# Bank evictions issued inside the projection, PSUM tiles of their own for the routing tables, and a branch hint

## The chip, the cores and the metric

One Trainium2 chip, of which the kernel uses one core. The metric is the device time of one execution in microseconds. The core's engines run side by side, each with its own instruction stream in program order: TensorE (PE, matmul; PEld is its weight load), VectorE (DVE), ScalarE (ACT), GpSimd (POOL) and SyncE (SP, which here issues most DMA transfers). An engine waits for another one on semaphores.

## The reference

One layer on 512 tokens of width 1024: a mixer (gated linear recurrence in four heads beside a convolution of 31 taps), then a mixture of 16 experts of which two are chosen for each token.

```python
u = _modulate(x, sh1, sc1)
# mixer: one input projection into q, f, i, og, ca, cgt (512 columns each)
q, f, i, og, ca, cgt = jnp.split(u @ w_in + b_in, [H, 2 * H, 3 * H, 4 * H, 4 * H + C], axis=-1)
o = _hgrn2(q, f, i, lb)                      # silu(q); chunks of 64, decays exp(cumsum log f)
h_a = rmsnorm(o) * norm_w * silu(og)
a = conv31(ca * sigmoid(cgt)) + conv_b       # causal, channel by channel
h_b = silu(_layernorm(a) * conv_g + conv_bb)
x = _post_ln(ALPHA * x + g1 * (concat(h_a, h_b) @ w_out + b_out), ln1_g[l], ln1_b[l])
# experts: router, one group of four per token, top-2 inside it, SwiGLU
x = _post_ln(ALPHA * x + g2 * _moe(_modulate(x, sh2, sc2), ...), ln2_g[l], ln2_b[l])
```

## The kernel before

**The mixer** (`mixer`, L993) is written by hand in program order for every engine. Six projections `project(gi)` (L1194) of 512 columns each run one behind the other, in the order ca, cgt, f, q (gi = 3), the values i (gi = 4) and the gate og (gi = 5). A projection is four steps of 24 matmuls (128x128 by 512 columns) into four accumulators `pj`, and there are four `pj` banks in all. So the first matmul of a projection's accumulator m waits until the result of the projection before has left bank m. For gi = 3 that is the SiLU on ACT (L1341), for gi = 4 the addition of a bias on VectorE (L1429): four instructions each, both issued when `project` has returned.

Between the steps other work is issued: `between(st)` behind each step (for gi = 4 `values`, which calls `decays(st)`, L1347, the exponentials of head st and the scaled q and k of head st - 1, and two products of the conditioning matrix, `more_ada`; for gi = 5 `heads(st)`, L1494: scores with predicated copies on VectorE, states, three `more_ada`). After it `fill` (L1183) issues convolution taps. VectorE has 23 taps for each of four channel groups and one sum behind each group, ACT and POOL share 8 more. `fill` decides by counters: `Load` (L976) adds an assumed cost to each engine's counter at each instruction, and taps are issued while VectorE's counter is a given distance behind TensorE's:

```python
        v.at = max(v.at, pe.at - 8.0)
        while dve and (n > 0 or v.at < pe.at - ahead):
            dve.pop(0)()
            n -= 1
```

`ahead` is 1.5, or 5 for steps 2 and 3 of gi = 4 (`AHEAD`, L910). At the end of `project` VectorE's and ACT's counters are set to at least TensorE's (L1201). What is left of the taps is issued by `fill(200)` (L1560).

**The branch.** Behind the second head, `check` computes a flag, and `heads(2)` calls `general` (L1862), which reads the flag into a register on four engines and jumps over a slow exact computation of the scores if the flag is 0. With these inputs it is 0.

**The tables.** Behind the mixer, `moe` (L462) computes on TensorE and VectorE the tables that say which token goes to which slot (`router.tables`, L280, `weight_tables`, L315, `small`, L219), and beside them expert 0's first product (`between`, L508, into `pg`). All this uses four PSUM tiles `pz` of two banks each: the tables take turns in the four banks of `pz0` and `pz1`, `pg` and `pt` are the two halves of `pz2`, `ph` and `po` those of `pz3`. The framework keeps order between instructions by tile. `turned_rows` (L481) transposes the next rows into `pt`, and `modulate` (L336) reads them. Then one block with code of its own for each engine and hand-written semaphores runs the experts (from L572), on the same tiles. TensorE's part begins with two semaphore increments (L576), register loads (`load`, L582) and a mark (`mark`, L606) for which SP's weight loads wait.

Of the kernel before, what the change touches and what calls it, by code (L numbers as in the profile page):

```python
# [458 lines left out]
        return (w[bass.ds(at, 1), :, :].rearrange("o r n -> (o r) n") for w in self.w)  # L459


def moe(nc, tc, K, work, psum, W, n2d, zd, out):  # L462


    v, g, s, pe = nc.vector, nc.gpsimd, nc.scalar, nc.tensor
    st = K.st
    z, y, skip = ([W.gu(x, t) for t in range(4)] for x in (16, 17, 15))
    whole, lower, upper = slice(0, D), slice(0, 512), slice(512, D)

    pz = [psum.tile([128, 2, 512], F32, name=f"pz{t}", bufs=1) for t in range(4)]  # L470
    pg = pz[2][:, 0, :].rearrange("p (u n) -> p u n", u=2)
    pt = pz[2][:, 1, :].rearrange("p (c h r) -> p c h r", c=4, h=2)
    ph, po = pz[3][:, 0, :], pz[3][:, 1, :]
    n2h = n2d.rearrange("t (h c) -> (t h) c", h=2)

    def gather(i, to):
# [32 lines left out]
        for k in todo.get(i, ()):  # L509
            up(pe, W.gu(0, k), st.XT0, 2, k)  # L510

    banks = [pz[t][:, i, :] for t in range(2) for i in range(2)]

    def bank():
        banks.append(banks.pop(0))
        return banks[-1]

    with tc.manual_schedule():

        v.memset(ph, 0.0)  # L520
        K.router.tables(bank, between)
        gather(1, st.XS)
        K.router.weight_tables(bank)
        s.activation(st.SL, pg[:, 0, :], AF.Silu)
        v.tensor_tensor(st.HB, pg[:, 1, :], st.SL, op=OP.mult)
        turned_rows()
        modulate(v, K, st.XT, pt)
        K.router.small(bank)

    names = ["u", "s", "e", "v", "t", "h", "pv", "pg", "x", "g", "xf", "d", "o", "z", "fg", "fd", "zl", "ln", "v2"]  # L530
    names += [f"ga{i}" for i in range(2)] + [f"sc{i}" for i in range(3)]

    names += ["ob", "fp", "fa", "fm", "fq", "fw", "fr", "fc", "fk", "fo", "fb", "st"] + [f"z{t}" for t in range(4)]
    sem = {n: tc.alloc_semaphore("moe_" + n) for n in names}

    full_g = [[tc.alloc_semaphore(f"moe_g{i}{k}") for k in range(4)] for i in range(3)]
# [35 lines left out]
    with tc.tile_critical():  # L572
        with nc.Block() as block:  # L573
            @block.tensor
            def _(pe):
                pe.sem_inc(sem["e"], 1)  # L576
                pe.sem_inc(sem["x"], 1)

                rows = [pe.alloc_register(f"moe_rows{i}") for i in range(3)]

                def load(x, at):
                    pe.reg_load(rows[x % 3], K.cnt[0:1, at:at + 1] if isinstance(at, int) else K.cnt[0:1, bass.ds(at, 1)])  # L582
# [118 lines left out]

            @block.vector
            def _(v):
                def turned():
                    take(v, "t")
                    v.tensor_copy(st.hT, ph[:, 0:256]).then_inc(sem["h"], 1)  # L706
# [200 lines left out]
SH = (0, -1, -1)  # L907
PR = 2
WARM = 12
AHEAD = {(4, 3): 5, (4, 2): 5}  # L910
W4 = 3
WB = 3
NACT = 8
# [57 lines left out]
def col(K, nm, i):  # L971
    c = K.c0[nm] + i
    return K.cols[:, c:c + 1]
# [19 lines left out]
def mixer(nc, tc, K, I, psum, P, modd, spill, n2d, zd):  # L993
# [197 lines left out]
        while act and act[0].m <= summed[0] + 1 and s.at < pe.at and g.at < pe.at:  # L1191
            act.pop(0)()

    def project(gi, channel_major, between=None, within=None):  # L1194
        out = [pj() for _ in range(4)]
        for st in range(4):
            step(gi * 4 + st, out, channel_major, within)
            if between:
                between(st)
            fill(0, AHEAD.get((gi, st), 1.5))  # L1200
        v.at = max(v.at, pe.at)  # L1201
        s.at = max(s.at, pe.at)
        return out
# [132 lines left out]
            v.tensor_tensor_scan(f_, K.smask, a_, 0.0, op0=OP.mult, op1=OP.add)  # L1336
            bs.append(f_.rearrange("p (c i) -> p c i", c=NCH))

    pq = project(3, True, between=logs)
    for h in range(4):  # L1340
        s.activation(q_[h], pq[h], AF.Silu, bias=col(K, "b_in", h))  # L1341
    dec = P[0].tile([128, 4, NCH], F32, name="dec")
    ext = P[0].tile([128, 4, 2, NCH], F32, name="ext")

# [79 lines left out]
    SC = q4pair(2, 3)  # L1424
    for h in range(4):
        g.memset(SC[h], 0.0)
    pv = project(4, False, between=values)
    for t, p in enumerate(pv):
        v.tensor_tensor(vt[t], p, vbias[0], op=OP.add)  # L1429
    decays(4)  # L1430

    exm = P[0].tile([128, 1], F32, name="exm")
# [33 lines left out]
    def turned(h):  # L1466
        pk = ms()
        for t in range(4):
            sl = slice(t * 128, (t + 1) * 128)
            pe.transpose(pk[:, sl], X[:, 4 + h, sl], K.ident)  # L1470
        kTs[h] = t2()
        s.activation(kTs[h], pk, AF.Copy)
# [21 lines left out]
    def heads(st):  # L1494
        if st == 2:
            general(nc, tc, K, ms, bad, spill, SC, t2)
        turned(st)
        if st < 2:
            scores(2 * st)
            scores(2 * st + 1)  # L1500
        if st == 1:
            check()
        fill(4)
        states(st)
        more_ada((3, 3, 3, 2)[st])
# [356 lines left out]
def general(nc, tc, K, ms, bad, spill, SC, t2):  # L1862
# [2 lines left out]

    v, g, s, pe = nc.vector, nc.gpsimd, nc.scalar, nc.tensor
    flag = nc.values_load(bad[0:1, 0:1], engines=(ET.PE, ET.Activation, ET.DVE, ET.Pool), min_val=0, max_val=1)
    with tc.If(flag > 0):  # L1868
        for h in range(4):
            v.memset(SC[h], 0.0)  # L1870
        for h in range(4):
# [53 lines left out]
def hybrid(tc, ctx, I, out):  # L1925
# [29 lines left out]
    with tc.tile_pool(name="tb", bufs=1, reuse_waits="tile") as tb, tc.tile_pool(name="wp", bufs=1, side="right", reuse_waits="tile") as wp:  # L1955
        moe_tables(K, tb)
        nc.gpsimd.dma_start(K.g2q, bass.AP(tensor=modd.tensor, offset=modd.offset + 2 * 512, ap=[[256, 4], [0, 32], [1, 256]]))
        nc.gpsimd.dma_start(K.g2h, bass.AP(tensor=modd.tensor, offset=modd.offset + 2 * 512, ap=[[512, 2], [0, 64], [1, 512]]))
        W = Weights(nc, K, wp, X4, I["w_gate"][0], I["w_up"][0], I["w_down"][0])
        with tc.manual_schedule():  # L1960
            for x in range(3):
                W.static(x)
            nc.sync.dma_start(K.st.ln2g, bcast_rows(I["ln2_g"], D))
            nc.sync.dma_start(K.st.ln2b, bcast_rows(I["ln2_b"], D))
        with tc.tile_pool(name="mp", bufs=1, space=PSUM, reuse_waits="tile") as mp, tc.tile_pool(name="mw", bufs=1, reuse_waits="tile") as mw:
            moe(nc, tc, K, mw, mp, W, n2d, zd, out)

# [1 line left out]
_INS = ["x", "c", "ada_w", "ada_b", "w_in", "b_in", "hgrn_norm_w", "conv_w", "conv_b", "conv_ln_g", "conv_ln_b",  # L1969
# [22 lines left out]
```

## Time and profile before

| | us |
|---|---|
| median of 3 runs | 696.8 (695.91 to 701.67) |
| the profiled execution | 703.01 |
| its span, first to last instruction | 701.2 |
| TensorE busy in the span | 588.2 (84%) |
| VectorE busy | 349.2 (50%) |
| GpSimd busy | 254.5 (36%) |
| ScalarE busy | 167.0 (24%) |

All times in the rows are those of the one profiled execution, from its first instruction on. A busy share over the whole span says little here, since the stages have different limits: the mixer's projections run from 21 to about 228 us, the output projection until 330, router and tables until 388, the experts until 692. What is read is which engine waits in a stage, and what ended the wait.

### The profile page before, as it was taken

Reading aid. Unit: us, or ns where it says so; the run is one execution under the profiler, and the core shown is the slowest. Engines: PE = TensorE matmul, PEld = TensorE weight load, DVE = VectorE, ACT = ScalarE, POOL = GpSimd, SP = SyncE. Lnnn points to the kernel's source line nnn. Section 1 sums busy time; section 2 is a strip of 40 time slices with the busy share of each in tenths; the row PEclk is TensorE's granted clock in tenths of the full one; section 3 lists DMA queues with packets and bytes.
Section 4 is the critical chain, followed back from the end, with each engine's and each line's share of the span. In section 5 each row is a group of like instructions: output and inputs, shape, how many; then the busy total and the mean of one; then the engine's idle time right before and its main releaser. Section 6 shows DMA issues by size and latency. Waiting matters only on the chain. (4 is left out here: it accounts for less than half of the span.)

```text
span 701.2 us, 10474 instructions
## 1 busy us (share of the span) xinstructions
PE 588.2 (84%) x3499; PEld 319.1 (46%) x3500; DVE 349.2 (50%) x694; ACT 167.0 (24%) x253; POOL 254.5 (36%) x209
## 2 busy tenths in 40 slices
PE   4899999793996787998765888999997799999970
PEld 2578878562664344676522243333332233343430
DVE  6447587999467665577764131222221122321356
ACT  1433567542310214224501010101010010110112
POOL 2245695977620222365600232222222112132215
PEclk9999999897988678899886799999998999999985
DMA  8953223595234567769990799973799997699953
GB/s 279 356 180 121 91 91 98 164 340 179 76 119 156 178 212 275 252 226 302 395 330 28 275 341 381 378 279 60 239 371 390 382 376 265 166 379 384 344 157 120
DMA packets 78784, 170.68 MB, mean 243 GB/s; under 512 B 8866, under 2 KB 18031, under 8 KB 78718
## 3 DMA queue, kind: packets, MB, share of 16 engines
q1 hardware_dynamic: 69456, 149.19, 59.8%
q0 software_dynamic: 9136, 20.80, 10.9%
q8 instruction: 22, 0.36, 0.2%
q14 instruction: 28, 0.23, 0.1%
q10 hardware_dynamic: 142, 0.09, 0.0%
HBM read 154.96 MB, written 15.34 MB: 243 GB/s over the span
## 5 line engine op out<-in xcount | busy, mean ns | idle before, releaser
L819 POOL DMA_INDIRECT zd<-flat,dst x25 | 39.9, 1597 | 204.2 <-POOLq L541 195.8
L492 PE MATMUL pz<-wt,flat 128*32 128x256 f32 (+1 forms) x672 | 93.9, 493 | 6.1 <-PEq L541 5.9
L989 POOL TENSOR_TENSOR wL<-w,wH 128x1024 fp32r<-128x1024 f32 x30 | 74.4, 2483 | 58.1 <-ACT wH L989 58.1
L989 PE MATMUL pj<-wH,U 128*128 128x512 f32 x224 | 76.7, 414 | 16.2 <-DVE q L989 10.9
L501 PE MATMUL pz<-wt,flat 128*64 128x512 f32 (+1 forms) x544 | 84.0, 515 | 2.6 <-PEq L541 1.7
L989 PE MATMUL pj<-U,wH 128*128 128x512 f32 x256 | 81.0, 395 | 4.5 <-DVE U L989 3.0
L492 PE MATMUL pz<-R,flat 128*64 128x512 f32 (+1 forms) x416 | 77.3, 547 | 7.8 <-PEq L541 6.3
L989 DVE SCALAR_TENSOR_TENSOR mx<-R,convw,mx 128x512 f32<-128x512 f32 x88 | 66.4, 754 | 6.2 <-DVEq L1868 3.5
L679 ACT ACTIVATE flat<-pz 128x256 f32<-128x256 f32 x25 | 9.6, 384 | 239.8 <-ACTq L541 239.8
L989 PEld LDWEIGHTS pj<-wH,U 128*128 128x128 f32 x224 | 44.4, 198 | 36.0 <-issue 21.3
L492 PEld LDWEIGHTS pz<-wt,flat 128*32 128x32 f32 (+1 forms) x672 | 32.7, 125 | 51.3 <-issue 45.8
L989 PEld LDWEIGHTS pj<-U,wH 128*128 128x128 f32 x256 | 47.6, 188 | 17.0 <-DVE U L989 4.4
L711 DVE TENSOR_TENSOR flat<-pz,flat 128x256 f32<-128x256 f32 x25 | 10.6, 425 | 88.6 <-DVEq L541 82.6
L706 DVE COPY flat<-pz 128x256 f32<-128x256 f32 x26 | 11.1, 425 | 81.0 <-DVEq L541 61.1
L989 PE MATMUL pj<-U,wL 128*128 128x512 f32 x128 | 50.1, 392 | 0.0
L501 PEld LDWEIGHTS pz<-wt,flat 128*64 128x64 f32 (+1 forms) x544 | 27.4, 128 | 44.1 <-issue 40.4
L478 POOL DMA_INDIRECT flat<-n2d,idx_i x28 | 27.8, 994 | 48.7 <-DVE flat L264 23.1
L989 PE MATMUL pj<-wL,U 128*128 128x512 f32 x112 | 45.4, 405 | 0.0
L492 PEld LDWEIGHTS pz<-R,flat 128*64 128x64 f32 (+1 forms) x416 | 24.8, 131 | 44.1 <-issue 42.2
L989 POOL TENSOR_TENSOR R<-R 128x512 f32<-128x512 f32 x28 | 39.0, 1396 | 14.3 <-ACT R L989 12.9
L989 ACT ACTIVATE wH<-w 128x1024 fp32r<-128x1024 f32 x30 | 31.5, 1055 | 24.7 <-PE pj L989 11.4
L726 DVE SCALAR_TENSOR_TENSOR flat<-pz,X,g2h 128x512 f32<-128x512 f32 x18 | 13.5, 751 | 38.5 <-DVEq L541 38.5
(389 smaller groups left out, 816.2 us busy)
## 6 DMA issues: line engine op xcount, KB each, us to landing
wt<-in_w_down_dram SPq DMA_DIRECT2D x60, 512.0 KB, 7.2
wt<-in_w_gate_dram SPq DMA_DIRECT2D x80, 256.0 KB, 6.7
wt<-in_w_up_dram SPq DMA_DIRECT2D x80, 256.0 KB, 7.0
q<-in_ada_w_dram SPq DMA_DIRECT2D x28, 512.0 KB, 7.7
w<-in_w_in_dram SPq DMA_DIRECT2D x24, 512.0 KB, 3.8
aw<-in_ada_w_dram SPq DMA_DIRECT2D x20, 512.0 KB, 5.6
R<-in_w_gate_dram SPq DMA_DIRECT2D x40, 256.0 KB, 6.3
R<-in_w_up_dram SPq DMA_DIRECT2D x40, 256.0 KB, 6.0
```

Source lines behind the costliest of these rows:

```text
L478: return g.indirect_dma_start(out=to, out_offset=None, in_=n2h, in_offset=bass.IndirectOffsetOnAxis(ap=K.idx[:, i:i + 1], axis=0))
L492: i = eng.matmul(pg[m * j:m * j + m, :, 0:cw], xT[:, c, h, 0:m], w[:, :, cw * j:cw * j + cw], start=k == 0, stop=k == 7)
L501: i = eng.matmul(po[m * q:m * q + m, 0:dw], st.hT[:, c * 128 + j * m:c * 128 + j * m + m], W.dn(x, f)[:, dw * q:dw * q + dw], start=f == 0 ...
L679: s.activation(st.SL, pg[:, 0, :], AF.Silu).then_inc(sem["s"], 1)
L706: v.tensor_copy(st.hT, ph[:, 0:256]).then_inc(sem["h"], 1)
L711: v.tensor_tensor(st.HB, pg[:, 1, :], st.SL, op=OP.mult).then_inc(sem["e"], 1)
L726: v.scalar_tensor_tensor(st.o[j % 3][:, :256 * n], po[:, :256 * n], w[:, j:j + 1], g2, op0=OP.mult, op1=OP.mult).then_inc(sem["o"], 1)
L819: g.indirect_dma_start(out=zd.rearrange("r (q c) -> (r q) c", c=dw), out_offset=bass.IndirectOffsetOnAxis(ap=dst[:, j:j + 1], axis=0), in_ ...
L989: return f(out, *a, **k)
```

## The change

It has five parts. `project` takes a function `last`, called behind the matmuls of step 3 and ahead of `between` and `fill`; the four SiLUs of gi = 3 (`take_q`) and the four additions of gi = 4 (`take_v`) are passed in so. The distance 5 for step 2 of gi = 4 goes, so that step has 1.5. The branch of `general` gets a label, and on TensorE and VectorE a hint is written behind `turned(1)` that its jump is likely taken. The tables get a PSUM pool of their own that is closed behind them, with a one-bank tile each for `pg`, `pt` and two for the tables in turn; the eight banks `pz` for the experts come from a new pool behind it. The memset of `ph` moves from the head of the tables into VectorE's part of the block, with one more for the bank of `pg`, and TensorE waits for both (`pw`) ahead of its register loads.

```diff
--- before.py
+++ after.py
@@ -459,18 +459,17 @@
         return (w[bass.ds(at, 1), :, :].rearrange("o r n -> (o r) n") for w in self.w)
 
 
-def moe(nc, tc, K, work, psum, W, n2d, zd, out):
+def moe(nc, tc, K, ctx, work, W, n2d, zd, out):
 
 
     v, g, s, pe = nc.vector, nc.gpsimd, nc.scalar, nc.tensor
     st = K.st
     z, y, skip = ([W.gu(x, t) for t in range(4)] for x in (16, 17, 15))
     whole, lower, upper = slice(0, D), slice(0, 512), slice(512, D)
-
-    pz = [psum.tile([128, 2, 512], F32, name=f"pz{t}", bufs=1) for t in range(4)]
-    pg = pz[2][:, 0, :].rearrange("p (u n) -> p u n", u=2)
-    pt = pz[2][:, 1, :].rearrange("p (c h r) -> p c h r", c=4, h=2)
-    ph, po = pz[3][:, 0, :], pz[3][:, 1, :]
+    first = ExitStack()
+    psum = first.enter_context(tc.tile_pool(name="mp", bufs=1, space=PSUM, reuse_waits="tile"))
+    pg = psum.tile([128, 2, 256], F32, name="pg", bufs=1)
+    pt = psum.tile([128, 4, 2, 64], F32, name="pt", bufs=1)
     n2h = n2d.rearrange("t (h c) -> (t h) c", h=2)
 
     def gather(i, to):
@@ -509,15 +508,8 @@
         for k in todo.get(i, ()):
             up(pe, W.gu(0, k), st.XT0, 2, k)
 
-    banks = [pz[t][:, i, :] for t in range(2) for i in range(2)]
-
-    def bank():
-        banks.append(banks.pop(0))
-        return banks[-1]
-
+    bank = lambda: psum.tile([128, 512], F32, name="tbl", bufs=2)
     with tc.manual_schedule():
-
-        v.memset(ph, 0.0)
         K.router.tables(bank, between)
         gather(1, st.XS)
         K.router.weight_tables(bank)
@@ -526,11 +518,18 @@
         turned_rows()
         modulate(v, K, st.XT, pt)
         K.router.small(bank)
+    first.close()
+
+    psum = ctx.enter_context(tc.tile_pool(name="mq", bufs=1, space=PSUM))
+    pz = [psum.tile([128, 2, 512], F32, name=f"pz{t}", bufs=1) for t in range(4)]
+    pg = pz[2][:, 0, :].rearrange("p (u n) -> p u n", u=2)
+    pt = pz[2][:, 1, :].rearrange("p (c h r) -> p c h r", c=4, h=2)
+    ph, po = pz[3][:, 0, :], pz[3][:, 1, :]
 
     names = ["u", "s", "e", "v", "t", "h", "pv", "pg", "x", "g", "xf", "d", "o", "z", "fg", "fd", "zl", "ln", "v2"]
     names += [f"ga{i}" for i in range(2)] + [f"sc{i}" for i in range(3)]
 
-    names += ["ob", "fp", "fa", "fm", "fq", "fw", "fr", "fc", "fk", "fo", "fb", "st"] + [f"z{t}" for t in range(4)]
+    names += ["ob", "fp", "fa", "fm", "fq", "fw", "fr", "fc", "fk", "fo", "fb", "st", "pw"] + [f"z{t}" for t in range(4)]
     sem = {n: tc.alloc_semaphore("moe_" + n) for n in names}
 
     full_g = [[tc.alloc_semaphore(f"moe_g{i}{k}") for k in range(4)] for i in range(3)]
@@ -577,6 +576,8 @@
                 pe.sem_inc(sem["x"], 1)
 
                 rows = [pe.alloc_register(f"moe_rows{i}") for i in range(3)]
+
+                take(pe, "pw")
 
                 def load(x, at):
                     pe.reg_load(rows[x % 3], K.cnt[0:1, at:at + 1] if isinstance(at, int) else K.cnt[0:1, bass.ds(at, 1)])
@@ -701,6 +702,10 @@
 
             @block.vector
             def _(v):
+
+                v.memset(ph, 0.0)
+                v.memset(pz[2][:, 0, :], 0.0).then_inc(sem["pw"], 1)
+
                 def turned():
                     take(v, "t")
                     v.tensor_copy(st.hT, ph[:, 0:256]).then_inc(sem["h"], 1)
@@ -907,7 +912,7 @@
 SH = (0, -1, -1)
 PR = 2
 WARM = 12
-AHEAD = {(4, 3): 5, (4, 2): 5}
+AHEAD = {(4, 3): 5}
 W4 = 3
 WB = 3
 NACT = 8
@@ -1191,10 +1196,13 @@
         while act and act[0].m <= summed[0] + 1 and s.at < pe.at and g.at < pe.at:
             act.pop(0)()
 
-    def project(gi, channel_major, between=None, within=None):
+    def project(gi, channel_major, between=None, within=None, last=None):
+
         out = [pj() for _ in range(4)]
         for st in range(4):
             step(gi * 4 + st, out, channel_major, within)
+            if st == 3 and last:
+                last(out)
             if between:
                 between(st)
             fill(0, AHEAD.get((gi, st), 1.5))
@@ -1336,9 +1344,11 @@
             v.tensor_tensor_scan(f_, K.smask, a_, 0.0, op0=OP.mult, op1=OP.add)
             bs.append(f_.rearrange("p (c i) -> p c i", c=NCH))
 
-    pq = project(3, True, between=logs)
-    for h in range(4):
-        s.activation(q_[h], pq[h], AF.Silu, bias=col(K, "b_in", h))
+    def take_q(pq):
+        for h in range(4):
+            s.activation(q_[h], pq[h], AF.Silu, bias=col(K, "b_in", h))
+
+    project(3, True, between=logs, last=take_q)
     dec = P[0].tile([128, 4, NCH], F32, name="dec")
     ext = P[0].tile([128, 4, 2, NCH], F32, name="ext")
 
@@ -1424,9 +1434,12 @@
     SC = q4pair(2, 3)
     for h in range(4):
         g.memset(SC[h], 0.0)
-    pv = project(4, False, between=values)
-    for t, p in enumerate(pv):
-        v.tensor_tensor(vt[t], p, vbias[0], op=OP.add)
+
+    def take_v(pv):
+        for t, p in enumerate(pv):
+            v.tensor_tensor(vt[t], p, vbias[0], op=OP.add)
+
+    project(4, False, between=values, last=take_v)
     decays(4)
 
     exm = P[0].tile([128, 1], F32, name="exm")
@@ -1495,6 +1508,8 @@
         if st == 2:
             general(nc, tc, K, ms, bad, spill, SC, t2)
         turned(st)
+        if st == 1:
+            tc.mark_branch_hint_location("general", "LikelyTaken", engines=[ET.PE, ET.DVE])
         if st < 2:
             scores(2 * st)
             scores(2 * st + 1)
@@ -1865,7 +1880,7 @@
 
     v, g, s, pe = nc.vector, nc.gpsimd, nc.scalar, nc.tensor
     flag = nc.values_load(bad[0:1, 0:1], engines=(ET.PE, ET.Activation, ET.DVE, ET.Pool), min_val=0, max_val=1)
-    with tc.If(flag > 0):
+    with tc.If(flag > 0, label="general"):
         for h in range(4):
             v.memset(SC[h], 0.0)
         for h in range(4):
@@ -1962,8 +1977,8 @@
                 W.static(x)
             nc.sync.dma_start(K.st.ln2g, bcast_rows(I["ln2_g"], D))
             nc.sync.dma_start(K.st.ln2b, bcast_rows(I["ln2_b"], D))
-        with tc.tile_pool(name="mp", bufs=1, space=PSUM, reuse_waits="tile") as mp, tc.tile_pool(name="mw", bufs=1, reuse_waits="tile") as mw:
-            moe(nc, tc, K, mw, mp, W, n2d, zd, out)
+        with ExitStack() as st, tc.tile_pool(name="mw", bufs=1, reuse_waits="tile") as mw:
+            moe(nc, tc, K, st, mw, W, n2d, zd, out)
 
 # ---- launch: one core; inputs and outputs as the reference has them ----
 _INS = ["x", "c", "ada_w", "ada_b", "w_in", "b_in", "hgrn_norm_w", "conv_w", "conv_b", "conv_ln_g", "conv_ln_b",
```

## Rows read from the trace of the kernel before

**Rows 1.** Stretch: us; busy of PE, PEld, DVE, ACT, POOL; clock; DMA.

```profile
160.00:170.90 10.90, 0.02 (x1) 0.05 (x1) 10.76 (x13) 3.95 (x6) 10.80 (x8) 0.71 0.58 198
```

**Rows 2.** TensorE's timeline: start, us, instruction, [idle before, what ended it].

```profile
170.88 0.76 PE L989 MATMUL pj<-wH,U 128*128 128x512 f32 x1 [10.91 <-DVE q L989]
216.77 1.09 PE L989 MATMUL ms<-ident,X 128*128 128x128 f32 x4 [4.97 <-DVEq L1868]
233.25 0.55 PE L989 MATMUL mx<-q,t 64*128 64x128 f32 x1 [4.54 <-DVE cv L989]
235.23 1.93 PE L989 MATMUL pa<-aw,cc 128*32 128x512 f32 x8
```

**Rows 3.** VectorE's timeline, 155 to 182 us.

```profile
155.72 1.54 DVE L989 SCALAR_TENSOR_TENSOR mx<-R,convw,mx 128x512 f32<-128x512 f32 x2
166.24 3.91 DVE L989 SCALAR_TENSOR_TENSOR mx<-R,convw,mx 128x512 f32<-128x512 f32 x5
170.05 2.48 DVE L989 TENSOR_TENSOR q<-pj,bb 128x512 f32<-128x512 f32 x4
172.52 1.29 DVE L989 TENSOR_TENSOR q<-q,t 128x512 f32<-128x512 f32 x2
181.00 1.00 DVE L989 COPY_PREDICATED q<-R,ms 128x128 f32<-128x128 uint8 x4 [7.19 <-PE ms L989]
```

**Rows 4.** ACT's timeline around the SiLUs of q.

```profile
125.05 1.32 ACT L989 ACTIVATE R<-R,convw 128x512 f32<-128x512 f32 x2
127.92 2.41 ACT L989 ACTIVATE q<-pj,cols 128x512 f32<-128x512 f32 x4
```

**Rows 5.** VectorE's timeline, 196 to 233 us.

```profile
196.93 1.00 DVE L989 COPY_PREDICATED q<-R,ms 128x128 f32<-128x128 uint8 x4 [6.95 <-PE ms L989]
216.72 6.30 DVE L989 SCALAR_TENSOR_TENSOR mx<-R,convw,mx 128x512 f32<-128x512 f32 x8 [3.50 <-DVEq L1868]
226.02 6.29 DVE L989 SCALAR_TENSOR_TENSOR mx<-R,convw,mx 128x512 f32<-128x512 f32 x8
```

**Rows 6.** The branch's line, sequencers (q): count, ns, first and last start.

```profile
L1868 ACTq COMPARE_BRANCH  x1: 45/45/45, 202.0 to 202.0; - x1
L1868 ACTq EVENT_SEMAPHORE  x1: 17/17/17, 202.5 to 202.5; - x1
L1868 PEldq COMPARE_BRANCH  x1: 6685/6685/6685, 208.5 to 208.5; - x1
L1868 DVEq COMPARE_BRANCH  x1: 72/72/72, 213.1 to 213.1; - x1
L1868 DVEq EVENT_SEMAPHORE  x1: 21/21/21, 216.6 to 216.6; - x1
```

**Rows 7.** Short stretches: columns as in rows 1, the clock third from the end.

```profile
170.00:172.00 2.00, 1.12 (x3) 0.95 (x4) 2.00 (x5) 0.00 (x0) 1.69 (x1) 0.50 0.55 131
230.00:232.00 2.00, 0.00 (x0) 0.00 (x0) 1.93 (x3) 0.70 (x1) 1.56 (x3) 1.00 0.17 34
234.00:236.00 2.00, 2.00 (x16) 1.20 (x16) 0.63 (x2) 0.00 (x0) 0.00 (x0) 0.50 0.96 264
```

**Rows 8.** Timelines of VectorE and TensorE in the tables.

```profile
361.51 0.48 DVE L520 MEMSET pz<- 128x512 f32 x1
374.81 0.69 DVE L276 TENSOR_TENSOR flat<-flat 128x512 bf16<-128x512 f16 x1
376.45 1.41 PE L322 MATMUL pz<-flat 128*64 128x32 f16 x24 [2.65 <-DVE flat L312]
381.38 1.12 PE L483 MATMUL pz<-ident,flat 128*128 128x128 f32 x4 [2.55 <-DVE flat L525]
382.53 0.69 DVE L339 TENSOR_TENSOR flat<-pz,scT 128x512 f32<-128x512 f32 x1 [1.21 <-PE pz L483]
```

**Rows 9.** Register loads at the block's entry, columns as in rows 6.

```profile
L548 DVEq TENSOR_LOAD <-cnt_i x1: 325/325/325, 386.2 to 386.2; - x1
L582 PEldq TENSOR_LOAD <-cnt_i x16: 298/306/320, 386.5 to 663.0; - x16
```

## The prediction

> **What bounds the kernel now.** I read the table of stretches first. In the stretch behind the mixer's fifth projection TensorE is busy 0.02 of 10.90 us while VectorE is busy 10.76 [rows 1]. So there the kernel waits for VectorE, not for arithmetic on TensorE. TensorE's own timeline then names what ends its long pauses: 10.91 us by a VectorE write of `q`, 4.97 us by VectorE's queue at the branch, 4.54 us by the last convolution sum `cv` [rows 2]. All three are VectorE, so I read VectorE's timeline last. In [rows 3] the reader sees the order that causes the first pause: two convolution taps (155.72), then `decays(3)` until 166.24, five more taps, and only at 170.05 the four additions `q<-pj,bb` that empty the four `pj` banks. TensorE starts 0.83 us behind the first of them. Behind them VectorE runs out of work until 181.00.
>
> **The plan of the taps.** `fill` decides by counters how many taps are issued behind each step, so the change moves taps too. I replayed the counters by hand with their costs from the code: a tap 0.662, a step 24 x 0.215 = 5.16, an `ada_mul` 1.29, `decays` 1.64 for h = 0 and 3.12 after, all counters 0 at the start of project(4). Behind steps 0 to 3 the matmul counter stands at 7.74, 15.48, 23.22, 30.96, and the rule (stop 1.5 short, 5 short for the last two) gives 7, 7, 2, 5 items; for the last, VectorE's counter is lifted to 30.96 - 8 = 22.96 first. The trace has the 2 [rows 3], and the tap that ends before 170.05 is the fifth. With the change step 2 stops 1.5 short: 17.15 to 21.72, 7 items. At step 3 the four additions (2.65) and `decays(3)` are counted before `fill`: 21.78 + 2.65 + 3.12 = 27.55, over 25.96: 0 items. So the sum stays 7, but all stand ahead of the additions and `decays(3)` stands behind them.
>
> **Part 1, `take_v`: 8.9 us.** The additions now stand behind 7 taps that start at 155.72. A tap takes 6.29 / 8 = 0.786 us [rows 5], so 155.72 + 5.50 = 161.2 instead of 170.05 [rows 3]. TensorE starts at 162.0 instead of 170.88 [rows 2]: 8.9 us. What is late next: the same work, `decays(3)` and `decays(4)`, is now behind the additions, and queued behind it are the predicated copies of `scores(0)`, for which TensorE waits in `states(0)`. Before, all of it was over at 172.52 + 1.29 = 173.8; the amount of work is the same, so 173.8 is the late bound. The copies, at 181.00 before, would be wanted at 172.1. At the late bound that costs 1.7 us for the first, so 7.2 is the lower end. The upper end is about 11: TensorE's clock stands at 0.50 in 170 to 172, behind the long pause [rows 7], and a shorter pause may spare up to 2 us of that first step. I take 8.9, because `decays(3)` now has idle time in front of its late users.
>
> **Part 2, four taps into idle time: 3.1 us.** At the end of a group VectorE's counter is set level with TensorE's. Before, the additions were counted after that; now they are not, so in project(5) the counter is 2.65 lower. In `heads(0)` it reads 39.26 where `fill` runs up to 41.56: 4 taps, where before it read 41.91 and issued none. They land where VectorE waited 6.95 us for TensorE (the pause before 196.93, [rows 5]): cost nothing while that pause lasts, 3.1 us if it were gone. Later counters are level again, so the 4 taps are missing at the end of the list, among the eight at 226.02 [rows 5]. TensorE waited 4.54 us for the sum behind those eight [rows 2], so 4 x 0.786 = 3.1 us are gained, bounds 0 and 4.5.
>
> **Part 3, the hint: 3.0 us.** The flag is 0, so every engine jumps over the body of `general`. ACT's branch stands at 202.0 and its next event at 202.5; VectorE's branch takes 72 ns at 213.1 and its next event stands at 216.6; TensorE's branch takes 6.7 us [rows 6]. I read the two long ones as waits for the code behind the jump. They end within the pause of 3.50 us on VectorE [rows 5], and TensorE, held until 216.77 [rows 2], is released by VectorE. If the code is there in time, VectorE's pause becomes ACT's 0.5 us: 3.0 us. VectorE works from there to the sum of the last tap, so this passes on whole, and TensorE's 6.7 us started at 208.5 and must be cut as well, or it holds `turned(2)` until 215.2, which TensorE's later slack covers in part. Bounds: 0 and 3.5. The instruction that writes the hint is not in this trace; an event instruction of 17 or 21 ns is the nearest row [rows 6], so it is nothing. [...]
>
> **Part 4, the clock: 1.9 us.** [...] So `states(3)` and two ada products, 233.25 to 237.16 [rows 2], run at half speed after a pause of 4.54 us. With parts 2 and 3 that pause is about 1 us, and this work falls where the clock was still up: half of 3.9 us. Bounds 0 and 7 (the slow stretch goes on behind these rows). I take 1.9, the row that the pause is nearest to.
>
> **Part 5, the tables: 1.7 us.** The memset of `ph` leaves VectorE's chain (0.48 us long, the next starts 0.4 later): 0.4 [rows 8]. The weight tables' matmul waited 2.65 us, to the end of L312, which reads the other bank of the same tile; its own input is ready when L276 ends, 374.81 + 0.69 = 375.5, so it starts 0.9 earlier. `turned_rows` (L483) waited 2.55 us for L525, which reads the other half of `pz2`; with `pg` and `pt` apart it is done early, and VectorE's 1.21 us of waiting for it at L339 goes [rows 8]. Together 2.5. Against it stands the new wait `pw`: VectorE enters the block at 386.2 and needs 0.4 + 0.48 us for the two memsets, so TensorE may go on at about 387.1; its first register load stood at 386.5 [rows 9]. Queued behind that wait are all of TensorE's loads and the first mark, for which SP's expert loads wait. Later by 0.6, with the semaphore 0.8. Net 1.7, bounds 0 and 2.5.
>
> **Part 6, `take_q`: 0.** The four SiLUs go ahead of the convolution copies on ACT: 125.05 instead of 127.92 [rows 4], so project(4) starts 2.9 us earlier, and SP's spill of `q` and the ada loads behind it too. It hides behind VectorE: the additions at 161.2 depend on VectorE's list alone, and TensorE had finished before that. If that cover were gone it would be worth 2.9.
>
> **The sum.** 8.9 + 3.1 + 3.0 + 1.9 + 1.7 = 18.6 us. Behind 260 us I see nothing with a time of its own: the experts' loads from the fourth on start on TensorE's mark in the block, so they move along with it. Span 701.2 - 18.6 = 682.6; the profiled execution 703.0 becomes 684.4. That execution was 6.2 us above the median of 696.8, so the median becomes 678.2.
>
> **The rivals.**
> [...]
> *The gain of part 1 is taken back*: VectorE becomes the bound of project(5), because `decays(3)` under load runs on past 173.8 (it took 9 us before, from the end of two taps near 157.2 to 166.24 [rows 3]) and the four taps of part 2 then stand in TensorE's way. Parts 1 and 2 shrink from 12.0 to some 3: about 687. The pause up to 181.00 speaks against it.
> *The clock gives more*: the slow stretch behind 233 comes out half fast and the step at 162 as well, 7 us more: 671.
> [...]
>
> **Chances.** All terms as told 0.50 (own range 674 to 683); hint without effect 0.20; more from the clock 0.10; gain taken back 0.15; slower 0.05. The likeliest gives 678.2. The range runs from 670 to 688, leaving out the slower case, part of the taken-back one and the tail of the clock. One per cent, about what a measurement here can tell from no change, is 7 us: below 689.8 is faster. The first three cases and two thirds of the fourth lie there: 0.85; within one per cent 0.10; slower 0.05.
>
> **What the changed kernel's profile would show.** Part 1: TensorE's pause before project(5) ends at about 162 with the additions directly behind seven taps. Part 2: four taps behind the first `states`, and four taps instead of eight ahead of the last sum. Part 3: VectorE's pause at the branch of 0.5 us, and TensorE's branch far below 6.7. Part 4: clock 1.00 at `states(3)`. Part 5: no wait for L312 and L525, and a wait of TensorE at the new `take` of about 0.8. The prediction is wrong if the copies of `scores(0)` wait for VectorE by more than 2 us, or if the span between the last sum and the first expert grows.

## The result and the profile after

| kernel | median us | lowest to highest | runs |
|---|---|---|---|
| before, beside the changed kernel | 696.36 | 694.16 to 701.67 | 4 |
| changed | 675.28 | 674.49 to 675.74 | 4 |
| changed, second time on another occasion | 674.32 | 673.77 to 675.86 | 6 |

The ratio to the kernel before is 0.9685 (0.963 to 0.9741), the second time 0.9704 (0.9667 to 0.9741): about 21 us faster. The profiled execution took 675.64 us, its span 673.9. Against the 703.01 us of the profiled execution before that is 27.4 us, 6 more than the medians give. So the kernel before was profiled a second time, unchanged (`e0_before`): 693.67 us, span 691.9. What differs between those two profiles of one kernel is no effect of the change, and the stretches below are taken from the second one.

TensorE's timeline of the changed kernel (start, us, instruction, [idle before, what ended it]), beside [rows 2]:

```profile
126.24 0.50 PE L994 MATMUL pj<-wH,U 128*128 128x512 f32 x1 [2.04 <-ACT q L994]
162.47 0.76 PE L994 MATMUL pj<-wH,U 128*128 128x512 f32 x1 [3.54 <-DVE q L994]
207.09 0.63 PE L994 MATMUL ms<-ident,X 128*128 128x128 f32 x4 [2.12 <-DVEq L1883]
220.41 0.34 PE L994 MATMUL mx<-q,t 64*128 64x128 f32 x1 [2.15 <-DVE cv L994]
```

The first row is the start of project(4); the other three are the pauses of [rows 2]. They are there again, ended by the same three writers, and each is shorter: 3.54 us instead of 10.91 ahead of project(5), 2.12 instead of 4.97 at the branch, 2.15 instead of 4.54 ahead of `states(3)`. VectorE's timeline shows why, beside [rows 3, 5]:

```profile
156.24 5.50 DVE L994 SCALAR_TENSOR_TENSOR mx<-R,convw,mx 128x512 f32<-128x512 f32 x7
161.64 2.48 DVE L994 TENSOR_TENSOR q<-pj,bb 128x512 f32<-128x512 f32 x4
173.28 1.00 DVE L994 COPY_PREDICATED q<-R,ms 128x128 f32<-128x128 uint8 x4 [4.14 <-PE ms L994]
182.48 3.12 DVE L994 SCALAR_TENSOR_TENSOR mx<-R,convw,mx 128x512 f32<-128x512 f32 x4
190.13 1.00 DVE L994 COPY_PREDICATED q<-R,ms 128x128 f32<-128x128 uint8 x4 [4.53 <-PE ms L994]
207.04 6.30 DVE L994 SCALAR_TENSOR_TENSOR mx<-R,convw,mx 128x512 f32<-128x512 f32 x8 [0.59 <-DVEq L1883]
216.34 3.12 DVE L994 SCALAR_TENSOR_TENSOR mx<-R,convw,mx 128x512 f32<-128x512 f32 x4
```

The additions stand directly behind seven taps. Four taps have moved to 182.48, ahead of a wait for TensorE, and four instead of eight are left at 216.34. The pause at the branch is 0.59 us instead of 3.50.

Where the time went, stretch by stretch, from the second profile of each kernel. Each stretch runs from one marked instruction to the next; the first scan of the logs is VectorE's first scan instruction, in project(3), `conv turn` is the first transposition behind `outputs`, L168 the first transposition of the tables.

| stretch, us | before | changed | gained |
|---|---|---|---|
| start to the first scan of the logs | 110.52 | 111.41 | -0.89 |
| to the start of project(5) | 59.42 | 50.55 | 8.87 |
| to `turned(1)` | 23.04 | 24.98 | -1.94 |
| to `turned(2)` | 22.16 | 19.68 | 2.48 |
| to `states(3)` | 16.48 | 13.31 | 3.17 |
| to `conv turn` | 11.78 | 10.31 | 1.47 |
| to L168 | 107.62 | 104.85 | 2.77 |
| to TensorE's first mark | 28.57 | 24.95 | 3.62 |
| to the end | 312.31 | 312.96 | -0.65 |
| span | 691.9 | 673.0 | 18.9 |

### The profile page after: what moved, and what is told of

The parts are those of the page before. It is cut to its first block, busy times and chain, and to the rows that moved or that the text cites. A ratio compares the mean times of both kernels' runs of the same rounds, so it can differ in the third digit from the quotient of the medians.

```text
span 673.9 us, 10476 instructions
## 1 busy us (share of the span) xinstructions
PE 577.5 (86%) x3499; PEld 314.0 (47%) x3500; DVE 344.0 (51%) x695; ACT 166.7 (25%) x253; POOL 254.4 (38%) x209
## 5 line engine op out<-in xcount | busy, mean ns | idle before, releaser
L491 PE MATMUL pz<-R,flat 128*64 128x512 f32 (+1 forms) x384 | 68.1, 534 | 6.4 <-PEq L540 6.4
L500 PEld LDWEIGHTS pz<-wt,flat 128*64 128x64 f32 (+1 forms) x544 | 27.4, 129 | 44.3 <-issue 40.7
L491 PEld LDWEIGHTS pz<-R,flat 128*64 128x64 f32 (+1 forms) x384 | 22.3, 129 | 40.9 <-issue 39.0
```

The lines of the kernel that those rows point to most:

```text
L491: i = eng.matmul(pg[m * j:m * j + m, :, 0:cw], xT[:, c, h, 0:m], w[:, :, cw * j:cw * j + cw], start=k == 0, stop=k == 7)
L500: i = eng.matmul(po[m * q:m * q + m, 0:dw], st.hT[:, c * 128 + j * m:c * 128 + j * m + m], W.dn(x, f)[:, dw * q:dw * q + dw], start=f == 0 ...
```

## Experiments

Medians of the kernel before beside the runs: 695.2 us for `e1` to `e3`, 696.27 for `e5` to `e8`, 695.4 for `e4`, `e9`, `e10` and `e11_after`.

**The hint taken away: `e1_nohint`.**

```diff
-        if st == 1:
-            tc.mark_branch_hint_location("general", "LikelyTaken", engines=[ET.PE, ET.DVE])
```

> The changed kernel without the mark of the branch. If the hint is worth what the pauses show (VectorE's pause at the branch back from 0.59 to 3.5, TensorE's branch back from 0.41 to 6.7 us): 675.3 + 3 = 678. If the code would have been there anyway: 675.3 and a pause of 0.6. If the longer pause also brings the clock down in the stretch behind states(3), up to 8.9 us more: 687.

Measured 677.63 us (673.87 to 679.37), ratio 0.9772 (0.9734 to 0.9809): 2.4 us above the changed kernel, but the executions of the two overlap, so what the hint is worth is read from the stretch below. The branch's line in the changed kernel (engine's sequencer, operation, ns, start), then in this one:

```profile
L1883 PEldq COMPARE_BRANCH  x1: 408/408/408, 201.7 to 201.7; - x1
L1883 PEldq EVENT_SEMAPHORE  x1: 51/51/51, 205.0 to 205.0; - x1
L1883 DVEq COMPARE_BRANCH  x1: 84/84/84, 206.3 to 206.3; - x1
L1883 DVEq EVENT_SEMAPHORE  x1: 21/21/21, 206.9 to 206.9; - x1
```

```profile
L1881 PEldq COMPARE_BRANCH  x1: 6217/6217/6217, 197.1 to 197.1; - x1
L1881 DVEq COMPARE_BRANCH  x1: 72/72/72, 201.7 to 201.7; - x1
L1881 PEldq EVENT_SEMAPHORE  x1: 51/51/51, 203.4 to 203.4; - x1
L1881 DVEq EVENT_SEMAPHORE  x1: 21/21/21, 204.7 to 204.7; - x1
```

From VectorE's branch to its next event 0.6 us pass with the hint and 3.0 without; TensorE's branch takes 0.41 us with it and 6.2 without, and from its start to TensorE's next event 3.3 us pass with it and 6.3 without. So the hint works on both engines, though on TensorE not all of the 6.2 us go; what fills the 3.3 is not shown. The stretch from `turned(1)` to `turned(2)` takes 21.97 us here, 22.16 before and 19.68 changed: the hint is worth 2.3 to 2.5 us. (This kernel's profiled execution, 673.87 us, was its shortest: its first step of project(5) ran at a clock of 1.00, behind a pause of only 2.38 us, since project(4) had waited 2.27 us for a DMA. This comes up again under part 6.)

**The additions put back behind the projection: `e2_late_v`.**

```diff
-AHEAD = {(4, 3): 5}
+AHEAD = {(4, 3): 5, (4, 2): 5}
...
-    project(4, False, between=values, last=take_v)
+    take_v(project(4, False, between=values))
```

> The changed kernel with the four additions of the values issued behind project again, and with the distance 5 for step 2. By the sum of the prediction 8.9 for the pause and 3.1 for the four taps come back: 675.3 + 12 = 687.3; TensorE pauses about 11 us ahead of project(5) and eight taps stand ahead of the last sum. If half clock behind project(5) ate part of the first term, as the changed kernel's trace suggests (8.9 at the start of project(5), 6.8 left at its second step): 685. If the stretch behind states(3) falls to half clock as well: 693.

Measured 689.12 us (687.99 to 695.32), ratio 0.994 (0.9896 to 0.9983): 13.8 us above the changed kernel, where parts 1 and 2 of the forecast add up to 12.0. VectorE's additions and TensorE's start behind them, in the profile of this kernel:

```profile
169.68 2.48 DVE L994 TENSOR_TENSOR q<-pj,bb 128x512 f32<-128x512 f32 x4
170.51 0.77 PE L994 MATMUL pj<-wH,U 128*128 128x512 f32 x1 [13.06 <-DVE q L994]
```

That is the picture of before [rows 2, 3] with a pause that is longer still, 13.06 us, since TensorE now comes to it earlier. So two thirds of the whole gain hang on these four additions and the taps around them; the run undoes both and does not part them.

**The tables as before, the mixer changed: `e3_old_tables`.** `moe` with the `pz` tiles, the memset at its head and no `pw`; everything else as in the changed kernel.

> The mixer's part of the change alone (early results, distances, hint); tables, PSUM tiles and the memset as before. By the prediction 1.7 us are lost: 677.0. By the two traces more is lost: from the router's first matmul to the last cast of the tables the changed kernel gained 5.3 us, of which the wait on the memsets took 1.1 back: 675.3 + 4.2 = 679.5, because without the memset at their head VectorE's first table operations stand ahead of the modulation of expert 0's rows.

Measured 678.77 us (676.26 to 684.45), ratio 0.9804 (0.9748 to 0.986): the tables are worth 3.5 us by the medians, not 1.7, though these four executions lie 8 us apart. Firmer are the profiles: the stretch from L168 to the first mark takes 28.57 us before, 28.44 here and 25.16 in the first profile of the changed kernel, so 3.3. Where the surplus is, the next run shows.

**Only the memset moved: `e6_memset_late`** (the kernel before with this edit).

```diff
     with tc.manual_schedule():
-
-        v.memset(ph, 0.0)
         K.router.tables(bank, between)
...
         K.router.small(bank)
+        v.memset(ph, 0.0)
```

> The kernel before with one line moved: the memset of `ph` at the head of the tables stands behind the last table. Theory A (the scheduler's order: without a write of `ph` at the head, the weight and index preparations of VectorE go ahead of the first modulation of expert 0's rows): the preparations of L238 to L294 stand ahead of L339, and besides the 0.4 us of the memset some 2 us are gained, about 693 against 695.3. Theory B (the table's surplus came from the tables' own tiles alone): 0.4 us, 695.

Measured 692.67 us (687.94 to 700.16), ratio 0.9935 (0.9895 to 0.9975), 3.6 us below before. VectorE's timeline in the tables, first in the second profile of before, then in this kernel:

```profile
351.71 0.69 DVE L339 TENSOR_TENSOR flat<-ms,scT 128x512 f32<-128x512 f32 x1 [4.56 <-PE ms L168]
353.62 0.21 DVE L238 TENSOR_TENSOR flat<-flat 128x64 f32<-128x64 bf16 x1
```

```profile
348.21 0.21 DVE L238 TENSOR_TENSOR flat<-flat 128x64 f32<-128x64 bf16 x1
352.84 0.69 DVE L339 TENSOR_TENSOR flat<-ms,scT 128x512 f32<-128x512 f32 x1 [1.36 <-PE ms L168]
```

Before, VectorE waited 4.56 us for L168 and only then began to prepare the tables (L238). With the memset gone from the head, the preparation stands ahead of L339 and fills that wait, of which 1.36 us are left. The stretch from L168 to the last table's matmul (L229) shrinks from 25.19 to 22.18 us by this edit alone; the tiles of their own bring it to 20.70 in the changed kernel. At the first mark 2.4 us of the 3.0 are left (26.20 us from L168 instead of 28.57), since with the memset now last the mark comes 4.02 us behind L229 instead of 3.38. Theory A holds. Why the compiled order follows the place of one memset no profile says; that it does is shown by a kernel in which nothing else was edited.

**The stop behind step 2 put back: `e5_ahead5`.**

```diff
-AHEAD = {(4, 3): 5}
+AHEAD = {(4, 3): 5, (4, 2): 5}
```

> The changed kernel with the old stop of step 2 put back: `fill` stops 5 short behind it, so 2 taps instead of 7 stand ahead of the four additions that empty the banks of project(4). The other five go behind `decays(3)` (3, by the counters) and into `heads(0)` (2). Theory A (the seven taps are what project(5) still waits for): the additions go directly behind the last product of project(4), project(5) starts at about 159.5 instead of 162.47, its first step no longer follows a long pause, and the five taps cost nothing, because VectorE waited 4.14 and 4.53 us for TensorE behind them: 3 us from the earlier start and up to 2.6 us from the clock, about 671. Theory B (VectorE's list is the bound up to `cv`, so an earlier project(5) only waits later): no change from the changed kernel, 675.

Measured 680.82 us (679.23 to 683.72), ratio 0.9768 (0.9712 to 0.9824): 5.5 us above the changed kernel, so both theories fell. The first half of theory A came true: `turned(0)` comes 6.4 us sooner behind the first scan than in the changed kernel. Then it was lost. VectorE's and GpSimd's timelines of this kernel:

```profile
156.23 2.48 DVE L994 TENSOR_TENSOR q<-pj,bb 128x512 f32<-128x512 f32 x4
158.63 3.50 DVE L994 TENSOR_TENSOR t<-bb 128x512 f32<-128x512 f32 x2
158.74 2.85 POOL L994 TENSOR_TENSOR wL<-w,wH 128x1024 fp32r<-128x1024 f32 x1
166.74 2.33 DVE L994 SCALAR_TENSOR_TENSOR mx<-R,convw,mx 128x512 f32<-128x512 f32 x3
168.97 4.33 DVE L994 COPY dec<-t 128x8 f32<-128x8 f32 x1
170.79 7.24 POOL L994 TENSOR_TENSOR R<-R 128x512 f32<-128x512 f32 x5
176.63 0.77 PE L994 MATMUL ms<-q,t 64*128 64x128 f32 x2 [6.28 <-DVE q L994]
```

```profile
164.03 1.28 DVE L994 TENSOR_TENSOR t<-bb 128x512 f32<-128x512 f32 x2
```

The last row is the changed kernel's: its two `t<-bb` take 1.28 us and fall into a pause of GpSimd. Here they stand beside GpSimd's split of the weights and take 3.50 us; a copy of 8 columns takes 4.33 us, where the changed kernel's first such copy, in GpSimd's pause, takes 0.17. `decays(3)` takes 8.1 us (158.63 to 166.74) instead of 2.6, and TensorE waits 6.28 us for `decays(4)` and the copies of the scores. The taps (2.33 us for three, 0.78 each) and the additions `q<-pj,bb` are not slowed. So the longer waits follow the place of `decays` beside GpSimd; no run takes GpSimd's work away to show it alone. This is the rival "the gain of part 1 is taken back", in a neighbouring kernel.

**Idle matmuls ahead of `states(3)`: `e7_warm`** (the kernel before with this edit).

```diff
+        if st == 3:
+            idle = pa_()
+            for _ in range(16):
+                pe.matmul(idle, K.onesb, K.onesb[:, None, :].to_broadcast([128, 4, 128]), start=True, stop=True)
```

> The kernel before with 16 idle matmuls (128x512, into a bank nobody reads at that time) ahead of the products of `states(3)`, in the pause in which TensorE waits for the last convolution sum. Nothing else differs. Theory A (the clock term as predicted, `states(3)` and the two ada products behind it at half speed): 1.5 to 1.9 us, about 693.5. Theory B (the slow stretch goes on behind `outputs(0)`): 5 to 7 us, 689. Theory C (VectorE sets the time of this stretch whatever TensorE's clock): 695.3.

Measured 692.48 us (689.92 to 695.42), ratio 0.9934 (0.99 to 0.9967), 3.8 us below before. A stretch behind `states(3)` in the second profile of before, then in this kernel (us, busy of PE, PEld, DVE, ACT, POOL, the granted clock, DMA share and rate):

```profile
232.00:234.00 2.00, 2.00 (x18) 1.57 (x20) 0.29 (x1) 0.00 (x0) 0.00 (x0) 0.50 0.85 246
343.40:353.40 10.00, 7.35 (x32) 2.16 (x30) 4.35 (x23) 0.60 (x1) 0.00 (x0) 0.66 1.04 320
```

```profile
234.00:236.00 2.00, 2.00 (x23) 1.04 (x20) 1.08 (x4) 0.00 (x0) 0.00 (x0) 1.00 0.94 291
343.96:353.96 10.00, 6.75 (x35) 1.94 (x31) 5.43 (x26) 0.60 (x1) 0.00 (x0) 0.90 1.05 318
```

The first row of each: `states(3)` at 0.50 before and at 1.00 here. From `states(3)` to `outputs(0)` it is 2.05 us instead of 3.53, so 1.5 us, the low end of theory A. The second row of each is the same work of the router, 100 us later, which the edit does not touch: clock 0.90 instead of 0.66, and from `conv turn` to L168 105.17 us instead of 107.62. That is the other 2.4 us.

**Idle matmuls ahead of project(5): `e8_warm5`.**

```diff
     project(4, False, between=values, last=take_v)
+    idle = psum.tile([128, 512], F32, name="ms", bufs=2)
+    for _ in range(14):
+        pe.matmul(idle, K.onesb, K.onesb[:, None, :].to_broadcast([128, 4, 128]), start=True, stop=True)
```

> The changed kernel with 14 idle matmuls (128x512, into a bank that nobody reads then) between project(4) and project(5), in the pause of 3.54 us. Theory A (part 1 lost 2.6 us because the first step of project(5) ran at 0.50 behind that pause: 8.16 us, where the kernel without the hint took 5.55 for it with the clock up): turned(0) about 2.6 us earlier behind the start of project(5), all of it kept up to `cv` since VectorE waits for TensorE twice behind it (4.14 and 4.53 us): 672.7. Theory B (VectorE's list is the bound): 675.3.

Measured 678.26 us (676.43 to 680.61), ratio 0.9729 (0.9673 to 0.9784). The first step of project(5) took 5.53 us instead of 8.16, as theory A says, and `turned(2)` came 4.4 us sooner behind the first scan. But the median is 3 us above the changed kernel's. TensorE's timeline shows the new wait, of `states(2)`:

```profile
209.09 0.55 PE L994 MATMUL mx<-q,t 64*128 64x128 f32 x1 [6.55 <-DVE cv L994]
```

By the code, the counter of `fill` took the idle matmuls for work and dealt the taps out earlier, and `states(2)` got the bank that the last sum still used; with the counter set back, in the next run, this wait is gone. So the median says nothing on what the clock is worth, only how far such a plan reaches.

**The same with the counter set back: `e9_warm5b`**, and with `pw` later as well: **`e10_both`.**

```diff
+    at = pe.at
     ... (the lines of the run before)
+    pe.at = at
```

```diff
-                take(pe, "pw")
...
                 wait(pe, full_d[0], 64)
+                take(pe, "pw")
                 rest(0)
```

> The changed kernel with 14 idle matmuls in the pause ahead of project(5), as in the run before of this kind, but with TensorE's counter set back behind them, so that `fill` deals out the taps as in the changed kernel. (There the counter took them for work: eight taps went behind the first states, the last sum was done at 208.9, and states(2) waited 6.55 us for it, because the sum's bank was then dealt out to states(2).) Theory A (the clock's 2.6 us are worth having once the taps stay where they were): 672.7. Theory B (what TensorE gains in its first step it waits for VectorE later, whatever the plan): 675.3.

> The same with one more edit: TensorE's wait `pw` for the two memsets stands behind its two register loads and the wait for the first expert's weights, ahead of the first mark, which writes `ph`. Theory A (of the 4.24 us between the last table and the first mark 0.8 are the wait in front of the loads): 0.8 us less than without this edit, 671.9. Theory B (TensorE waits for the code or for the memsets anyway): no change from it.

Measured 675.41 us (670.33 to 677.9), ratio 0.9717 (0.9668 to 0.9766), and 674.16 us (670.58 to 676.09), ratio 0.969 (0.9648 to 0.9732); the changed kernel beside them 674.32. In the profile of `e9_warm5b` the first step takes 5.56 us, and from the first scan to `states(3)` it is 105.7 us instead of 108.5, so the 2.8 us are kept that far. (The step behind it, `turned(0)` to `turned(1)`, still takes 16.83 us, as in the changed kernel.) The medians don't show them: its executions scatter over 7.6 us, the changed kernel's over 2.1. Whether the idle matmuls cost something elsewhere is left open. In `e10_both` the time from L229 to the first mark is 3.51 us instead of 4.46: the wait cost 0.95 us in front of the loads, which is too little to be told apart in the medians.

**The SiLUs of `q` late again: `e4_late_q`.**

```diff
-    project(3, True, between=logs, last=take_q)
+    take_q(project(3, True, between=logs))
```

> The changed kernel with the four SiLUs of `q` behind `project(3)` again, so behind the convolution copies on ScalarE; the rest of the change stays. Theory A (the 2.9 us at the start of project(4) hide behind VectorE, as predicted): project(4) starts about 2.9 us later, the additions of `v` stand where they stood, 675. Theory B (the cover is not whole: a shorter pause ahead of project(5) or a later spill of `q` counts): up to 2.9 us more, 678.

Measured 671.14 us (670.13 to 672.77), ratio 0.9663 (0.9625 to 0.9701); the changed kernel beside it, with the expectation

> The changed kernel without an edit, for a second profile and so that the next three are compared on one chip. Every theory: 675 (0.9685 of the kernel before).

took 674.32 (673.77 to 675.86). The two do not overlap: undoing this one part makes the kernel 3.2 us faster, and it is the fastest of all here. Neither theory had that sign. TensorE's timeline of this kernel, then the stretch of the first step of project(5) in it (columns as above):

```profile
127.44 0.80 PE L994 MATMUL pj<-wH,U 128*128 128x512 f32 x1 [4.91 <-ACT q L994]
160.72 0.47 PE L994 MATMUL pj<-wH,U 128*128 128x512 f32 x1 [2.44 <-DVE q L994]
```

```profile
160.70:166.20 5.50, 5.47 (x24) 4.56 (x25) 5.50 (x12) 2.57 (x5) 3.21 (x4) 1.00 0.70 258
```

The same timeline and stretch in the second profile of the changed kernel:

```profile
161.96 0.77 PE L994 MATMUL pj<-wH,U 128*128 128x512 f32 x1 [5.04 <-DVE q L994]
```

```profile
162.00:170.00 8.00, 8.00 (x24) 6.41 (x25) 6.63 (x13) 3.96 (x6) 5.56 (x4) 0.66 0.20 76
```

Counted from the first scan, VectorE's list runs alike in both: the additions at 49.63 and 49.72 us, project(5) 50.46 and 50.55. TensorE starts project(4) 2.9 us later and therefore waits 2.44 us ahead of project(5) instead of 5.04. Behind the shorter pause the clock is 1.00, and 24 matmuls take 5.5 us; behind the longer one it is 0.66 over the step, and they take 8. The step after it, from `turned(0)` to `turned(1)`, differs too, first here, then in the changed kernel:

```profile
166.29:182.24 15.95, 15.18 (x103) 10.10 (x102) 11.44 (x25) 8.41 (x12) 15.46 (x12) 0.89 0.42 140
```

```profile
170.08:186.94 16.86, 16.39 (x103) 11.13 (x102) 10.30 (x23) 7.00 (x10) 15.14 (x11) 0.80 0.40 126
```

That is 0.9 us more at a lower clock. At `turned(1)` the difference is 3.6 us, and it is still 3.6 at the first mark.

## Why the prediction was right, and where its steps were not

The time forecast was 678.2 us with 670 to 688; it came out at 675.3, by the likeliest case. The sum of 18.6 us stands against 21.1 by the medians and 18.9 between the second profiles. That it agrees so closely is in part luck: part 1 kept 1.9 us less than told, part 5 gave 1.8 more, and 2.8 came from a stretch that the sum left out. One sum among the chances is wrong: the first three cases (0.80) and two thirds of the fourth (0.10) make 0.90, not the 0.85 given for "faster". The terms, in their own order:

**Part 1, 8.9 us: right to the tenth, and 1.9 given back.** 8.87 us at the start of project(5), by the seven taps that the replay of the counters gave; the two decays end 5 us behind the additions, and the scores' copies waited for TensorE (4.14 us), not for VectorE. The late bound held, with `decays(3)` in a pause of GpSimd, where it took 2.6 us; `e5_ahead5` shows it beside GpSimd's work, where it took 8.1 us, as it had taken 9 before the change. What the term missed is the clock behind the pause. It allowed up to 2 us more if the shorter pause spared the clock. The pause became 3.54 us (5.04 in the second profile), and the clock still fell. Of the 1.94 us that the table gives back up to `turned(1)`, 1.00 is in the step behind the pause (8.12 us instead of 7.12) and 0.94 in the one after it (16.86 instead of 15.92, clock 0.80 instead of 0.89). Two short stretches of the changed kernel, columns as above, show the step's start at 0.50 and its end:

```profile
162.00:164.00 2.00, 1.53 (x4) 1.27 (x5) 2.00 (x4) 0.00 (x0) 1.72 (x2) 0.50 0.93 362
168.00:170.00 2.00, 2.00 (x10) 1.60 (x10) 1.15 (x2) 1.35 (x2) 2.00 (x1) 0.99 0.00 0
```

**Part 2, 3.1 us: right.** Four taps at 182.48, four instead of eight at the end, 3.17 us by the table of stretches.

**Part 3, 3.0 us: right, 2.4 measured.** VectorE's pause is 0.59 us where 0.5 was told, but without the hint it would have been 3.00 (`e1_nohint`; 2.94 in the second profile of before) and not 3.50. The case "hint without effect" (0.20) is refuted: by the mark alone the pause is 0.59 us instead of 3.00, and TensorE's branch takes 0.41 us instead of 6.2. That the long waits at the branch were for the code behind the jump was the author's reading; no run shows what the engines waited for. Nothing of the case "slower" (0.05) appears: from the first mark to the end it is 312.3 us before and 313.0 changed, and the whole is 21 us faster.

**Part 4, 1.9 us: right in size, and for the stated reason.** The half speed before is that of [rows 7], 0.50 in 234 to 236 us against 1.00 in 230 to 232. `states(3)` now runs at 1.00, and the stretch behind it is 1.47 us shorter; `e7_warm` gets 1.5 us for the clock alone. The pause, told as about 1 us, was 2.15, and the clock stayed up all the same. The slow stretch that goes on behind these rows in the first profile of before belongs to that execution: it lasted 18.4 us there to `conv turn`, 11.8 in the second. So the bound of 7 was read from what that one execution had. The stretch of `states(3)` in the changed kernel:

```profile
220.00:222.00 2.00, 1.59 (x22) 1.12 (x22) 0.66 (x3) 0.24 (x1) 1.87 (x4) 1.00 0.14 21
```

**Part 5, 1.7 us: mis-sized, 3.3 to 3.6 measured.** The waits went as told. TensorE's timeline of the changed kernel, and VectorE's:

```profile
349.88 0.87 PE L322 MATMUL tbl<-flat 128*64 128x32 f16 x22 [0.81 <-DVE flat L276]
353.24 1.12 PE L482 MATMUL pt<-ident,flat 128*128 128x128 f32 x4 [1.64 <-DMA flat<-n2d,idx_i]
354.39 0.69 DVE L339 TENSOR_TENSOR flat<-pt,scT 128x512 f32<-128x512 f32 x1 [0.30 <-PE pt L482]
358.19 0.48 DVE L706 MEMSET pz<- 128x512 f32 x1 [1.39 <-issue]
360.87 0.19 PE L609 MATMUL pz<-onesb 128*32 128x1 bf16 x1 [4.27 <-PEq L540]
```

L322 waits for its own input L276, L483 (now L482) for its gathered rows, and L339 0.30 us instead of 1.21 [rows 8]. The tiles of their own gave 1.5 us (22.18 to 20.70), where 0.9 + 1.2 was told. `pw` cost 1.1 us instead of 0.8: from L229 to the mark 4.46 us against 3.38. The term that failed is the memset: taken as its 0.4 us in VectorE's chain, it moved the whole preparation of the tables into VectorE's wait for L168, 3.0 us with `e6_memset_late`. So 3.0 + 1.5 - 1.1 = 3.4.

**Part 6, 0: the wrong step, hidden by a right total.** The 2.9 us were indeed covered by VectorE. But "earlier and covered" was not free: it lengthened TensorE's pause ahead of project(5), from 2.44 us to 5.04 in the second profile (3.54 in the first), and the clock behind it fell from 1.00 to 0.66 over the step. `e4_late_q` shows it by the order, `e9_warm5b` by filling the pause, and the profile of `e1_nohint` by accident: a DMA made project(4) late by itself, the pause was 2.38 us, and the step took 5.55. The term should have been -3.2. The prediction had both halves, the pause in part 6 and the clock in part 1, and did not put them together.

**Missing from the sum: 2.8 us from `conv turn` to L168.** "Behind 260 us I see nothing with a time of its own" was wrong. The router's work, unchanged, runs at a higher clock. The stretch in the second profile of the changed kernel that answers to the one at 343.40 above (0.66):

```profile
330.24:340.24 10.00, 5.85 (x32) 2.18 (x30) 7.71 (x38) 0.60 (x1) 0.00 (x0) 0.89 1.08 312
```

Its clock is 0.89. `e7_warm` gets the same from idle matmuls 100 us earlier, `e6_memset_late`, whose mixer is that of before, does not (107.84 us). So it follows from the mixer's part and not from the tables. Over all 14 profiles this stretch takes 107.6 to 107.8 us in four (before twice, `e5_ahead5`, `e6_memset_late`), in all of which `states(3)` to `conv turn` was slow (11.8 us and more), and 104.9 to 105.6 in nine, in eight of which it took 10.3; `e2_late_v` (12.9, yet 105.2) and `e8_warm5` (10.3, yet 106.9) do not fit. By what path the clock of the router depends on work so far back is left open.

## What to carry to other kernels

Where one engine empties the banks of another and the other waits for it, try the emptying directly behind the last step in program order, and replay by hand whatever planner deals out the work around it: for the values that was two thirds of the gain, and it came out as replayed, while the same move for `q` cost 3.2 us. Work moved earlier on an engine that then waits anyway need not be free: look at the pause that it lengthens (here 2.44 to 5.04 us) and at the clock behind it (1.00 to 0.66), and test that part alone. A single profile of the kernel before can carry an accident of several us (here 703.01 us against 693.67); a second one costs little and tells which stretches are its own.

## What the runs showed of the hardware

- With the mark behind `turned(1)` (187.5 us) and the branches at 201.7 and 206.3, TensorE's branch takes 0.41 us instead of 6.2 to 6.7, its next event comes 3.3 us behind the branch's start instead of 6.3 to 6.7, and VectorE's pause there is 0.6 us instead of 2.9 to 3.5.
- Of VectorE's instructions that stand beside GpSimd's work in `e5_ahead5` some are stretched and others not: 1.75 us on the mean instead of 0.64 for `t<-bb`, 4.33 instead of 0.17 for the copy `dec<-t` of 8 columns, but 0.78 as ever for a tap (`mx<-R,convw,mx`). What parts the stretched from the others no run shows.
- TensorE at the start of project(5): granted clock 1.00 behind pauses of 2.38 us (`e1_nohint`) and 2.44 us (`e4_late_q`), and behind one that idle matmuls filled but for 1.60 us (`e9_warm5b`); 0.66 over the step behind pauses of 3.54 and 5.04 us (the two profiles of the changed kernel), in the first of them 0.50 from 162 to 164 us. The step of 24 matmuls takes 5.5 us in the first three and 8.1 to 8.2 in the other two; behind the pauses of 10.3 to 13.1 us in before, `e2_late_v`, `e6_memset_late` and `e7_warm` it took 7.1 to 7.8.
- The clock of a stretch can differ steadily between two kernels that do the same there: 0.66 (`e0_before`) or 0.89 and 0.90 (`e11_after`, `e7_warm`) in the router, 2.4 to 2.8 us.
